# Attention scores of a hybrid encoder layer: fp32 on halves of the array in place of split fp32 on all of it

## The chip, the cores and the metric

The kernel runs on one core of a Trainium2 chip. A core has a matrix engine (TensorE, PE in the profile), a vector engine (VectorE, DVE), a scalar engine (ScalarE, ACT), a general engine (GpSimd, POOL) and a queue engine (SyncE, SP) that issues most transfers. Each engine takes its instructions in the order of the program and waits on semaphores for the others. The time is the device time of one execution in microseconds; a kernel's figure is the median of its runs.

## The reference

One layer of an encoder over two sequences (g = 0 and 1) of 2048 tokens with 1024 channels. One projection of the normalised input feeds three branches: a long convolution (hyena), a short convolution (conformer) and attention of the tokens to 256 memory tokens. Their gated outputs are joined, projected out and normalised again. What the change touches is the attention:

```
def memory_attention(q, mem_n, w_kv):
    k, v = jnp.split(mem_n @ w_kv, 2, axis=-1)      # 256 memory tokens
    q = q.reshape(B, L, 4, 64); k = k.reshape(B, M, 4, 64); v = ...
    s = jnp.einsum('blhd,bmhd->bhlm', q, k) * (64 ** -0.5)
    p = jax.nn.softmax(s, axis=-1)
    o = jnp.einsum('bhlm,bmhd->blhd', p, v)
```

All is in fp32. There are four heads of 64 channels, so two heads fill the 128 partitions.

## The kernel before

The kernel works in three stages. **Projections** (0 to 1381 us): for each block of 128 output channels the weights and the input are split into a high and a low part in a faster fp32 form (fp32r), and three matmuls (lines 416 to 418) per chunk give nearly fp32 results. Beside them run background jobs: keys and values of the memory (`kv_background`), the conformer's convolution (lines 215 to 257), the hyena filter (lines 295 to 334). **Attention** (1381 to 1542 us): 16 blocks of two heads by 512 queries (2 sequences, 2 pairs of heads, 4 token chunks), interleaved with the first transform of the long convolution (lines 799 to 809), two of its steps around each block. **Transforms and output**: the other transforms (lines 815 to 834) to about 1720 us, and then the output projection (lines 931 to 951).

In the projection stage `xa_q` scales a block of queries by 1/8 out of PSUM and splits it: the high part by ACT (L522), the low part by DVE (L523), and stores high and low of each head with four transfers (L526) so that a later load gives, for one head, high parts on partitions 0 to 63 and low parts on 64 to 127. `kv_background`'s `store` splits the transposed keys in the same way (lines 574 to 578). The high part of a key stands on all 128 partitions, the low part on 64 with zeros below. One full-array matmul with the high keys then adds high x high and low x high, a second with the low keys adds high x low.

An attention block goes in two halves of 256 queries (index `u`), and a half in two tiles of 128 queries (index `t`). For each tile: four matmuls into one PSUM bank (L748, two heads by two), the maximum by DVE (L752), two exps with sums by ACT (L756), the reciprocal by DVE (L758), the product by POOL (L760), four transposes by PE (L763) and one copy out of PSUM (L765). After both tiles, four output matmuls (L770), each with 64 columns of the array: head 0 gives partitions 0 to 63, head 1 64 to 127. These are plain fp32. Two PSUM banks hold scores (`ms`), three transposes (`tr`), one outputs (`po`).

The order of the instructions on each engine is not the order of the code alone: the tile framework's scheduler, with its own model of times, takes from what is ready. So an edit of one job can move others.

Of the kernel before, what the change touches and what calls it, by code (L numbers as in the profile page):

```python
# [18 lines left out]
P = 128  # L19
# [83 lines left out]
def kernel(ctx: ExitStack, tc: tile.TileContext, a: dict):  # L103
# [8 lines left out]
    dram = ctx.enter_context(tc.tile_pool(name="dram", bufs=1, space=bass.MemoryType.DRAM))  # L112
    HD = [[dram.tile([P, L + 2 * CH], F32, name=f"hd{g}{c}") for c in range(2)] for g in range(2)]
    SZ = [[dram.tile([P, L], F32, name=f"sz{g}{c}") for c in range(2)] for g in range(2)]
    QS = [[dram.tile([2, 64, 2, L], F32R, name=f"qs{g}{c}") for c in range(2)] for g in range(2)]
    ZX = [[dram.tile([P, L], F32, name=f"zx{g}{c}") for c in range(2)] for g in range(2)]
    KB = [dram.tile([P, 2048], F32R, name=f"kb{g}") for g in range(2)]
# [71 lines left out]
    with ExitStack() as c1:  # L189
# [328 lines left out]

        def xa_q(g, i):
            def f(tb, ps):  # L520
                qh, ql = sm(TB, F32R), sm(TB, F32R)
                nc.scalar.activation(qh, ps, AF.Copy, scale=0.125)  # L522
                nc.vector.scalar_tensor_tensor(ql, ps, 0.125, qh.bitcast(F32), op0=ALU.mult, op1=ALU.subtract)  # L523
                for j, q in enumerate((qh, ql)):
                    for h in range(2):
                        nc.sync.dma_start(QS[g][i][j, :, h, tb * TB:(tb + 1) * TB].bitcast(F32),  # L526
                                          q[64 * h:64 * h + 64, :].bitcast(F32))
            return (COL_Q + i * P, f)

        def kv_background():  # L530
            st = {}

            def norm(g):
                st["m", g] = big().rearrange("p (k t) -> p k t", k=KC)
                normed(st["m", g], a["mt"][g], mems[g][0], 8)
                st["p", g] = ms(), ms()

            def fetch(k):
                raw, wh, wl = sm(), bt(TB, F32R), bt(TB, F32R)
                nc.sync.dma_start(raw, a["xa_w_kv"][0, k * P:(k + 1) * P, :])  # L540
                split(wh, wl, raw)
# [12 lines left out]

            def store(g):
                kv = bt()
                vt = bt()
                vv = vt.rearrange("p (i m c) -> p i m c", i=2, m=2)
                for s, ps in enumerate(st["p", g]):
                    ss = slice(s * 256, (s + 1) * 256)  # L560
                    nc.scalar.copy(kv[:, ss], ps[:, 0:256])
                    nc.vector.tensor_copy(vv[:, :, s, :], ps[:, 256:512].rearrange("p (i c) -> p i c", i=2))
                nc.sync.dma_start(VT[g], vt)
                pk = tr()
                for i in range(2):
                    for s in range(2):
                        nc.tensor.transpose(pk[:, i * 256 + s * P:i * 256 + (s + 1) * P],
                                            kv[:, s * 256 + i * P:s * 256 + (i + 1) * P], ident)
                kt = big(2048, F32R)
                kb = kt.rearrange("p (h q m) -> p h q m", h=4, q=2)  # L570
                for h in range(4):
                    r = slice(64 * (h % 2), 64 * (h % 2) + 64)
                    ro = slice(64 - 64 * (h % 2), 128 - 64 * (h % 2))
                    src = pk[r, (h // 2) * 256:(h // 2 + 1) * 256]
                    nc.scalar.copy(kb[r, h, 0, :], src)
                    nc.scalar.copy(kb[ro, h, 0, :], src)
                    nc.vector.tensor_tensor(kb[0:64, h, 1, :], src, kb[r, h, 0, :].bitcast(F32), op=ALU.subtract)
                    nc.gpsimd.memset(kb[64:128, h, 1, :].bitcast(F32), 0.0)
                nc.sync.dma_start(KB[g].bitcast(F32), kt.bitcast(F32))

            bgq.append(lambda: norm(0))
            bgq.append(lambda: (norm(1), fetch(0)))
            for k in range(KC):
                bgq.append(lambda k=k: (fetch(k + 1) if k < KC - 1 else None, accum(k)))
            for g in range(2):
                bgq.append(lambda g=g: store(g))
# [108 lines left out]
    with ExitStack() as c2:  # L695
# [12 lines left out]
        kvs = {}  # L708

        def load_kv(g):  # L710
            kt, vt = ((woh[0:2], woh[3]), (wol[0:2], wol[2]))[g]
            for i in range(2):
                nc.gpsimd.dma_start(kt[i], KB[g][:, i * 1024:(i + 1) * 1024])
            vt = vt.bitcast(F32)[:, 0:512]
            nc.gpsimd.dma_start(vt, VT[g])
            kvs[g] = ([t.rearrange("p (h q m) -> p h q m", h=2, q=2) for t in kt],
                      vt.rearrange("p (i m c) -> p i m c", i=2, m=2))

        qn = [0]

        def queries(g, i, tb):
            qt = (woh[2], wol[5])[qn[0] % 2]
            qn[0] += 1
            nc.gpsimd.dma_start(qt.rearrange("p (h t) -> p h t", h=2),
                                QS[g][i][:, :, :, tb * TB:(tb + 1) * TB].rearrange("q r h t -> (q r) h t"))
            return qt

        pn = [0]
# [5 lines left out]
        def attention(g, i, tb, qy):  # L734
            kb, vt = kvs[g]
            qt = qy
            y = t_out()
            nc.sync.dma_start(y, ZX[g][i][:, tb * TB:(tb + 1) * TB])
            o = po_()
            for u in range(2):  # L740
                pt = pts[pn[0] % 6]
                pn[0] += 1
                for t in range(2):
                    sc = ms()
                    for h in range(2):
                        q0 = h * TB + u * 256 + t * P
                        for j in range(2):
                            nc.tensor.matmul(sc[:, h * 256:(h + 1) * 256], qt[:, q0:q0 + P], kb[i][:, h, j, :],  # L748
                                             start=j == 0, stop=j == 1)
                    mx = tiny.tile([P, 2], F32, tag="mx", name=nm("mx"))  # L750
                    se = tiny.tile([P, 2], F32, tag="se", name=nm("se"))
                    nc.vector.tensor_reduce(mx, sc.rearrange("p (h m) -> p h m", h=2), axis=AX.X, op=ALU.max,  # L752
                                            negate=True)
                    e = eps_[2 * u + t]
                    for h in range(2):
                        nc.scalar.activation(e[:, h * 256:(h + 1) * 256], sc[:, h * 256:(h + 1) * 256], AF.Exp,  # L756
                                             bias=mx[:, h:h + 1], accum_out=se[:, h:h + 1])
                    nc.vector.reciprocal(se, se)  # L758
                    ev = e.rearrange("p (h m) -> p h m", h=2)
                    nc.gpsimd.tensor_tensor(ev, ev, se.unsqueeze(2).broadcast_to([P, 2, 256]), op=ALU.mult)  # L760
                    tp = tr()
                    for k in range(4):
                        nc.tensor.transpose(tp[:, k * P:(k + 1) * P], e[:, k * P:(k + 1) * P], ident)  # L763
                    tv = tp.rearrange("p (k t) -> p k t", k=4)
                    (nc.vector.tensor_copy if t else nc.scalar.copy)(pt[:, :, t * P:(t + 1) * P], tv)  # L765

                for m in range(2):
                    for h in range(2):
                        hs = slice(64 * h, 64 * h + 64)
                        nc.tensor.matmul(o[hs, u * 256:(u + 1) * 256], vt[:, i, m, hs], pt[:, 2 * h + m, :],  # L770
                                         start=m == 0, stop=m == 1)
# [231 lines left out]
```

## Time and profile before

| | |
|---|---|
| runs | 2136.59 us median of 3 (2136.57 to 2137.94) |
| profiled execution | 2141.23 us, of which the span from first to last instruction is 2139.4 us |
| TensorE busy | 2005.3 us, 94% of the span, 9058 matmul records and as many weight loads |
| VectorE, ScalarE, GpSimd busy | 59%, 36%, 42% |
| mean granted TensorE clock | 0.975 |

Busy time is the sum of the records of an engine. Records of matmuls overlap (a matmul is recorded from its start to its modelled end, while the next has long begun), so the time that a matmul holds the engine is the distance from one start to the next, which the chain of waits shows. PEld is the weight load, which runs ahead of the matmul where it can. Idle time is given with what ended it.

### The profile page before, as it was taken

To read this page: it belongs to the slowest core of one execution; us is meant where nothing else is said; L and a number is where in the kernel's file an instruction comes from. 1 tells how busy PE (TensorE), PEld (TensorE's weight loads), DVE (VectorE), ACT (ScalarE), POOL (GpSimd) and SP (SyncE) were. 2 spreads that over 40 slices of the span, in tenths; PEclk is the share of its full clock that TensorE was granted. 3 is DMA by queue.
4 is the path that set the end of the run, shared out by engine and by line. 5 is a ranking of instruction groups with operands and counts; after the bars stand their busy time and mean duration, and the time that the engine had idled before them with its cause. 6 is when DMAs were issued, how large, how long until landed. Compare 5 with 4: busy or idle time off the path is not lost.

```text
span 2139.4 us, 26345 instructions
## 1 busy us (share of the span) xinstructions
PE 2005.3 (94%) x9058; PEld 1573.6 (74%) x9058; DVE 1266.4 (59%) x1747; ACT 761.6 (36%) x1439; POOL 897.6 (42%) x857
## 2 busy tenths in 40 slices
PE   5999998987999999998999899999988899999998
PEld 4888876776787788886777778777533278888886
DVE  5756397978315464469585963177887624333443
ACT  5531212231424233232233244277687711111211
POOL 3423475655533211455554541266588711111111
PEclk9999999999999999999999999999999989999999
DMA  9643222331657323222222236698788776555562
GB/s 334 206 149 137 90 99 89 109 109 69 220 169 230 125 100 109 86 90 81 95 80 105 81 114 204 218 296 259 236 263 272 229 194 155 154 144 152 148 151 56
DMA packets 197886, 331.81 MB, mean 155 GB/s; under 512 B 53129, under 2 KB 74265, under 8 KB 194938
## 3 DMA queue, kind: packets, MB, share of 16 engines
q1 hardware_dynamic: 170938, 272.06, 41.0%
q10 hardware_dynamic: 21392, 46.18, 6.6%
q0 software_dynamic: 5424, 11.90, 2.1%
q8 instruction: 72, 1.18, 0.2%
q14 instruction: 60, 0.49, 0.1%
HBM read 199.45 MB, written 130.61 MB: 154 GB/s over the span
## 4 chain that ended last, share of the span: by engine, by line
PE 49%; DVE 8%; DMA 4%; ACT 2%; issue 2%; POOL 2%; SPq 1%; ACTq 0%; POOLq 0%; DVEq 0%
PE pj L418 6%; PE pj L416 6%; PE pj L417 6%; PE ms L948 5%; PE ms L950 5%; PE ms L949 5%; DVE bg L220 5%; PE tr L931 2%; PE tr L763 1%; PE po L770 1%; PE ms L748 1%; PE tr L815 1%; DMA in<-xf 1%; PE ms L333 1%; DMA in<-x1d 1%
## 5 line engine op out<-in xcount | busy, mean ns | idle before, releaser
L416 PE MATMUL pj<-xh,whi 128*128 128x512 f32 (+1 forms) x1728 | 673.3, 390 | 29.0 <-ACT big L481 8.6
L417 PE MATMUL pj<-xl,whi 128*128 128x512 f32 (+1 forms) x1728 | 672.8, 389 | 7.8 <-POOL xl L387 5.1
L418 PE MATMUL pj<-xh,wlo 128*128 128x512 f32 (+1 forms) x1728 | 671.4, 389 | 0.0
L220 DVE SCALAR_TENSOR_TENSOR bg<-bg,vb,bg 128x512 f32<-128x512 f32 x480 | 420.4, 906 | 10.9 <-POOL bg L215 5.7
L416 PEld LDWEIGHTS pj<-xh,whi 128*128 128x128 f32 x1728 | 333.2, 193 | 98.9 <-ACT big L481 9.9
L417 PEld LDWEIGHTS pj<-xl,whi 128*128 128x128 f32 x1728 | 333.5, 193 | 73.2 <-POOL xl L387 5.9
L418 PEld LDWEIGHTS pj<-xh,wlo 128*128 128x128 f32 x1728 | 333.6, 193 | 65.1 <-DMA wlo<-ws 0.4
L948 PE MATMUL ms<-wo,mh 128*128 128x512 f32 x512 | 207.1, 405 | 1.8 <-ACT mh L178 1.8
L949 PE MATMUL ms<-wo,mh 128*128 128x512 f32 x512 | 201.7, 394 | 0.0
L950 PE MATMUL ms<-wo,ml 128*128 128x512 f32 x512 | 199.5, 396 | 0.2 <-POOL ml L179 0.2
L439 DVE SCALAR_TENSOR_TENSOR sm<-sm,va,sm 128x448 f32<-128x448 f32 (+1 forms) x96 | 82.4, 859 | 161.7 <-POOL sm L437 131.8
L437 POOL TENSOR_SCALAR sm<-sm,va 128x448 f32<-128x448 f32 (+1 forms) x96 | 113.0, 1178 | 135.6 <-ACT sm L430 129.2
L458 POOL TENSOR_TENSOR big<-big,sm 128x448 f32<-128x448 f32 (+1 forms) x64 | 121.5, 1899 | 107.7 <-DVE sm L441 104.2
L951 DVE TENSOR_TENSOR xr<-xr,ms 128x512 f32<-128x512 f32 x64 | 44.0, 687 | 204.3 <-PE ms L950 203.3
L185 POOL TENSOR_TENSOR ss<-ss,mhalf 128x1 f32<-128x1 f32 x32 | 17.6, 550 | 315.9 <-DVE ss L184 315.9
L183 ACT ACTIVATE junk<-xr 128x1024 bf16<-128x1024 f32 x32 | 33.8, 1058 | 318.4 <-DVE xr L951 318.2
L430 ACT COPY sm<-pj 128x512 f32<-128x512 f32 x96 | 56.1, 584 | 211.1 <-PE pj L418 162.9
L948 PEld LDWEIGHTS ms<-wo,mh 128*128 128x128 f32 x512 | 97.5, 191 | 21.4 <-ACT mh L178 3.2
L950 PEld LDWEIGHTS ms<-wo,ml 128*128 128x128 f32 x512 | 96.8, 189 | 21.2 <-POOL ml L179 0.6
L949 PEld LDWEIGHTS ms<-wo,mh 128*128 128x128 f32 x512 | 97.4, 190 | 19.2
L179 POOL TENSOR_TENSOR wlo<-sm,whi 128x512 fp32r<-128x512 f32 x50 | 77.7, 1567 | 73.4 <-ACT whi L178 70.6
L822 POOL TENSOR_TENSOR z<-z,us 128x512 f32<-128x512 f32 x64 | 81.4, 1282 | 30.8 <-DVE us L821 27.2
(177 smaller groups left out, 2935.0 us busy)
## 6 DMA issues: line engine op xcount, KB each, us to landing
big<-in_xt_dram SPq DMA_DIRECT2D x32, 512.0 KB, 5.5
in<-x1d SPq DMA_DIRECT2D x128, 128.0 KB, 3.7
aa<-o ACTq DMA_DIRECT2D x64, 256.0 KB, 3.7
at<-aa SPq DMA_DIRECT2D x64, 256.0 KB, 4.1
out_dram<-xr ACTq DMA_DIRECT2D x64, 256.0 KB, 3.6
sm<-in_win_dram SPq DMA_DIRECT2D x52, 256.0 KB, 3.3
ws<-whi SPq DMA_DIRECT2D x52, 256.0 KB, 2.1
ws<-wlo SPq DMA_DIRECT2D x52, 256.0 KB, 4.1
```

The source lines that it names most:

```text
L179: (sub_eng or nc.gpsimd).tensor_tensor(lo, src, hi.bitcast(F32), op=ALU.subtract)
L220: nc.vector.scalar_tensor_tensor(st["a", c], st["h", c][:, k:k + TB], vb[:, 2 * k + c:2 * k + c + 1], st["a", c], op0=ALU.mult, op1=ALU.add)
L416: nc.tensor.matmul(ps[:, ts_], hi, xh[:, k, ts_], start=k == 0, stop=False)
L417: nc.tensor.matmul(ps[:, ts_], hi, xl[:, k, ts_], start=False, stop=False)
L418: nc.tensor.matmul(ps[:, ts_], lo, xh[:, k, ts_], start=False, stop=k == KC - 1)
L437: nc.gpsimd.tensor_scalar(ct[:, o:e], pt[:, o + 1:e + 1], w[1], va[:, 52 + ch:53 + ch], op0=ALU.mult, op1=ALU.add)
L439: nc.vector.scalar_tensor_tensor(ct[:, o:e], pt[:, o:e], w[0], ct[:, o:e], op0=ALU.mult, op1=ALU.add)
L458: nc.gpsimd.tensor_tensor(v, v, out, op=ALU.mult)
L822: nc.gpsimd.tensor_tensor(z, z, us, op=op)
L948: nc.tensor.matmul(po, mh[:, k, :], woh[k][:, hs], start=i == 0, stop=False)
L949: nc.tensor.matmul(po, mh[:, k, :], wol[k][:, hs], start=False, stop=False)
L950: nc.tensor.matmul(po, ml[:, k, :], woh[k][:, hs], start=False, stop=i == 7)
```

## The change

The split of queries and keys is dropped. Queries are scaled and stored once (one transfer per chunk), keys are copied once. A score matmul now takes 64 partitions: head 0 on partitions 0 to 63, head 1 on 64 to 127, each head in a PSUM bank of its own, in plain fp32. A bank holds one head by 256 queries (two tiles) instead of two heads by 128 queries, and so do the maximum, the exps, the product and the transposes that follow; the loops over `t` and `h` change places. The buffers that queries, keys and values are loaded into move, and loads are smaller: 256 KB instead of 512 KB for queries, 256 KB instead of 1 MB for keys.

```diff
         def xa_q(g, i):
             def f(tb, ps):
-                qh, ql = sm(TB, F32R), sm(TB, F32R)
-                nc.scalar.activation(qh, ps, AF.Copy, scale=0.125)
-                nc.vector.scalar_tensor_tensor(ql, ps, 0.125, qh.bitcast(F32), op0=ALU.mult, op1=ALU.subtract)
-                for j, q in enumerate((qh, ql)):
-                    for h in range(2):
-                        nc.sync.dma_start(QS[g][i][j, :, h, tb * TB:(tb + 1) * TB].bitcast(F32),
-                                          q[64 * h:64 * h + 64, :].bitcast(F32))
+                q = sm()
+                nc.scalar.activation(q, ps, AF.Copy, scale=0.125)
+                nc.sync.dma_start(QS[g][i][:, tb * TB:(tb + 1) * TB], q)
...
-                kt = big(2048, F32R)
-                kb = kt.rearrange("p (h q m) -> p h q m", h=4, q=2)
-                for h in range(4):
...
-                    nc.scalar.copy(kb[r, h, 0, :], src)
-                    nc.scalar.copy(kb[ro, h, 0, :], src)
-                    nc.vector.tensor_tensor(kb[0:64, h, 1, :], src, kb[r, h, 0, :].bitcast(F32), op=ALU.subtract)
-                    nc.gpsimd.memset(kb[64:128, h, 1, :].bitcast(F32), 0.0)
-                nc.sync.dma_start(KB[g].bitcast(F32), kt.bitcast(F32))
+                kt = bt()
+                nc.scalar.copy(kt, pk)
+                nc.sync.dma_start(KB[g], kt)
...
+                sc = ms(), ms()
                 for t in range(2):
-                    sc = ms()
                     for h in range(2):
-                        q0 = h * TB + u * 256 + t * P
-                        for j in range(2):
-                            nc.tensor.matmul(sc[:, h * 256:(h + 1) * 256], qt[:, q0:q0 + P], kb[i][:, h, j, :],
-                                             start=j == 0, stop=j == 1)
+                        r, q0 = slice(64 * h, 64 * h + 64), u * 256 + t * P
+                        nc.tensor.matmul(sc[h][:, t * 256:(t + 1) * 256], qt[r, q0:q0 + P], kb[r, i, :],
+                                         start=True, stop=True)
+                for h in range(2):
...
-                    nc.vector.tensor_reduce(mx, sc.rearrange("p (h m) -> p h m", h=2), axis=AX.X, op=ALU.max,
+                    nc.vector.tensor_reduce(mx, sc[h].rearrange("p (t m) -> p t m", t=2), axis=AX.X, op=ALU.max,
...
-                    for k in range(4):
-                        nc.tensor.transpose(tp[:, k * P:(k + 1) * P], e[:, k * P:(k + 1) * P], ident)
-                    tv = tp.rearrange("p (k t) -> p k t", k=4)
-                    (nc.vector.tensor_copy if t else nc.scalar.copy)(pt[:, :, t * P:(t + 1) * P], tv)
+                    for m in range(2):
+                        for t in range(2):
+                            k = 2 * m + t
+                            nc.tensor.transpose(tp[:, k * P:(k + 1) * P], e[:, t * 256 + m * P:t * 256 + (m + 1) * P],
+                                                ident)
+                    (nc.vector.tensor_copy if h else nc.scalar.copy)(
+                        pt[:, 2 * h:2 * h + 2, :], tp.rearrange("p (m t) -> p m t", m=2))
```

The change moves instructions on PE too. Lines have other numbers in the changed kernel: L732 are the scores (before L748), L737 the maximum (L752), L743 the reciprocal (L758), L750 the transposes (L763), L758 the outputs (L770), L787 and L793 to L795 the transform's transposes and matmuls (L799, L805 to L807). In the rows below `ms` is a score bank, `po` the output bank, `tr` and `pa` banks of transposes and transforms, `x4` four calls in a row; a plain fp32 call is one row here.

PE in the kernel before, in the second half of a block in the steady part of the attention stage: the scores of both tiles stand together.

```order
L799 MATMUL tr_10974<-ident,u_1514_10851 128x128 x4
L748 MATMUL ms_11075<-wo_9935,wo_9947 128x256 x4
L748 MATMUL ms_11093<-wo_9935,wo_9947 128x256 x4
L799 MATMUL tr_11008<-ident,u_1552_10997 128x128 x4
L770 MATMUL po_10888<-ynp,wo_9937 64x256 x4
L763 MATMUL tr_11047<-ident,ynp 128x128 x4
```

PE in the changed kernel, at the same place; bank 10903 is head 0 and bank 10904 head 1.

```order
L787 MATMUL tr_10806<-ident,u_1498_10691 128x128 x4
L732 MATMUL ms_10903<-wo_9824,wo_9833 128x256 x2
L758 MATMUL po_10728<-ynp,wo_9825 64x256
L787 MATMUL tr_10840<-ident,u_1536_10829 128x128 x4
L732 MATMUL ms_10904<-wo_9824,wo_9833 128x256 x2
L758 MATMUL po_10728<-ynp,wo_9825 64x256 x3
L750 MATMUL tr_10880<-ident,ynp 128x128 x4
```

The scores of the two heads are parted by an output matmul and four transposes, and the four output matmuls are parted into one and three.

PE in the kernel before, in the first half of the same block.

```order
L748 MATMUL ms_11035<-wo_9935,wo_9947 128x256 x4
L748 MATMUL ms_11053<-wo_9935,wo_9947 128x256 x4
L805 MATMUL pa_10871<-k_1519_10867,th_10858 128x512
L806 MATMUL pa_10871<-k_1519_10867,tl_10859 128x512
L807 MATMUL pa_10871<-k_1520_10868,th_10858 128x512
L805 MATMUL pa_10878<-k_1519_10867,th_10858 128x512
L806 MATMUL pa_10878<-k_1519_10867,tl_10859 128x512
L807 MATMUL pa_10878<-k_1520_10868,th_10858 128x512
L763 MATMUL tr_10941<-ident,ynp 128x128 x4
L770 MATMUL po_10888<-ynp,wo_9937 64x256 x4
```

PE in the changed kernel, in the first half of that block; bank 10867 is head 0 and bank 10868 head 1.

```order
L732 MATMUL ms_10867<-wo_9824,wo_9833 128x256 x2
L732 MATMUL ms_10868<-wo_9824,wo_9833 128x256 x2
L750 MATMUL tr_10778<-ident,ynp 128x128 x4
L758 MATMUL po_10728<-ynp,wo_9825 64x256
L793 MATMUL pa_10711<-k_1503_10707,th_10698 128x512
L794 MATMUL pa_10711<-k_1503_10707,tl_10699 128x512
L795 MATMUL pa_10711<-k_1504_10708,th_10698 128x512
L793 MATMUL pa_10718<-k_1503_10707,th_10698 128x512
L794 MATMUL pa_10718<-k_1503_10707,tl_10699 128x512
L795 MATMUL pa_10718<-k_1504_10708,th_10698 128x512
L750 MATMUL tr_10791<-ident,ynp 128x128 x3
L758 MATMUL po_10728<-ynp,wo_9825 64x256 x3
```

Here the scores stay together, head 0 twice and then head 1 twice, and the outputs are parted again.

DVE in the kernel before, at the end of the projections: the last low halves of queries (L523) stand ahead of the first maximum (L752).

```order
L616 COPY sm_9661<-ms_9657 128x512
L523 SCALAR_TENSOR_TENSOR sm_9817<-pj_9791,sm_9816 128x512
L523 SCALAR_TENSOR_TENSOR sm_9850<-pj_9824,sm_9849 128x512
L523 SCALAR_TENSOR_TENSOR sm_9883<-pj_9857,sm_9882 128x512
L523 SCALAR_TENSOR_TENSOR sm_9916<-pj_9890,sm_9915 128x512
L752 TENSOR_REDUCE mx_10015<-ms_10010 128x2
```

DVE in the changed kernel, at the same place (L604 is the transform's copy, before L616).

```order
L179 TENSOR_TENSOR bg_9564<-tr_9558,bg_9563 128x512
L604 COPY sm_9548<-ms_9544 128x512
L604 COPY sm_9571<-ms_9567 128x512
L737 TENSOR_REDUCE mx_9905<-ms_9899 128x2
L737 TENSOR_REDUCE mx_9918<-ms_9900 128x2
```

The four rows are gone, and the maxima of the first half block follow the transform's copies directly.

## Rows read from the trace of the kernel before

**Rows 1.** The page: engines (busy, share, count), and the chain that ended last.

```profile
PE 2005.3 (94%) x9058; PEld 1573.6 (74%) x9058; DVE 1266.4 (59%) x1747; ACT 761.6 (36%) x1439; POOL 897.6 (42%) x857
...
PE 49%; DVE 8%; DMA 4%; ACT 2%; issue 2%; POOL 2%; SPq 1%; ACTq 0%; POOLq 0%; DVEq 0%
```

**Rows 2.** Busy time by stretch: length, engines' busy us (count), granted clock, DMA share, GB/s.

```profile
76.00:306.00 230.00, 230.00 (x1078) 192.28 (x1076) 144.23 (x193) 60.65 (x115) 101.62 (x96) 1.00 0.36 124
1400.00:1496.00 96.00, 96.00 (x674) 75.27 (x673) 74.19 (x148) 74.82 (x238) 60.78 (x70) 1.00 0.94 276
...
1386.00:1390.00 4.00, 3.38 (x15) 2.80 (x14) 1.94 (x6) 2.04 (x8) 3.47 (x4) 0.50 0.99 321
```

**Rows 3.** The chain of waits through one attention block: start us, us, what.

```profile
1449.01 0.44 PE tr L763 x4
1449.45 0.96 PE ms L748 x8
1450.40 0.23 PE pa L805
...
1451.79 0.44 PE tr L763 x4
1452.23 1.01 PE po L770 x8
1453.24 0.59 PE tr L763 x4
1453.83 0.44 PE tr L799 x4
1454.27 0.96 PE ms L748 x8
1455.22 0.44 PE tr L799 x4
1455.66 1.01 PE po L770 x8
1456.67 0.59 PE tr L763 x4
...
1458.65 0.44 PE tr L763 x4
```

**Rows 4.** The chain behind the attention, and line 295's matmuls (min/median/max ns, starts).

```profile
1538.85 0.86 PE ms L829 x2
...
L295 PE MATMUL ms<-f,wf x48: 377/378/792, 697.9 to 1271.8; 128*128 128x256 f32 x32, 66*128 66x256 f32 x16
```

**Rows 5.** Lines 748 and 770: weight loads (min/median/max ns, first to last start).

```profile
L748 PEld LDWEIGHTS ms<-wo,wo x256: 186/190/338, 1380.9 to 1531.9; 128*128 128x128 f32 x128
...
L770 PEld LDWEIGHTS po<-ynp,wo x256: 132/136/138, 1393.4 to 1542.2; 128*64 128x64 f32 x128
```

**Rows 6.** PE's waits in the projections: waiting <- waited for, us, times, longest.

```profile
PE ms L228 <- ACT bg L178: 21.4, 3, 9.2
...
PE pj L416 <- ACT big L481: 8.6, 3, 4.3
...
PE pj L416 <- ACT sm L430: 6.5, 3, 3.6
...
PE pj L416 <- DVE sm L523: 4.8, 4, 1.7
```

**Rows 7.** PE's three longest waits from 1381 to 1545 us.

```profile
PE ms L748 <- ACT ynp L756: 2.2, 4, 0.9
PE ms L748 <- DVE sm L523: 0.9, 1, 0.9
PE tr L763 <- POOL ynp L760: 0.4, 1, 0.4
```

**Rows 8.** Line 523: its instructions, and what DVE was idle for before them (us, times).

```profile
L523 DVE SCALAR_TENSOR_TENSOR sm<-pj,sm x16: 680/691/693, 634.2 to 1382.0; 128x512 fp32r<-128x512 f32 x16
...
  ACT sm L522: 66.0, 8
```

**Rows 9.** Line 577, the subtractions of the key preparation.

```profile
L577 DVE TENSOR_TENSOR big<-tr,big x8: 404/418/427, 141.7 to 149.4; 64x256 fp32r<-64x256 f32 x8
```

More of the change, by code (lines that the diff above doesn't have):

```diff
@@ L114 @@
     SZ = [[dram.tile([P, L], F32, name=f"sz{g}{c}") for c in range(2)] for g in range(2)]
-    QS = [[dram.tile([2, 64, 2, L], F32R, name=f"qs{g}{c}") for c in range(2)] for g in range(2)]
+    QS = [[dram.tile([P, L], F32, name=f"qs{g}{c}") for c in range(2)] for g in range(2)]
     ZX = [[dram.tile([P, L], F32, name=f"zx{g}{c}") for c in range(2)] for g in range(2)]
-    KB = [dram.tile([P, 2048], F32R, name=f"kb{g}") for g in range(2)]
+    KB = [dram.tile([P, 512], F32, name=f"kb{g}") for g in range(2)]
     VT = [dram.tile([P, 512], F32, name=f"vt{g}") for g in range(2)]
@@ L568, in store @@
                                             kv[:, s * 256 + i * P:s * 256 + (i + 1) * P], ident)
-                kt = big(2048, F32R)
-                kb = kt.rearrange("p (h q m) -> p h q m", h=4, q=2)
-                for h in range(4):
-                    r = slice(64 * (h % 2), 64 * (h % 2) + 64)
-                    ro = slice(64 - 64 * (h % 2), 128 - 64 * (h % 2))
-                    src = pk[r, (h // 2) * 256:(h // 2 + 1) * 256]
-                    nc.scalar.copy(kb[r, h, 0, :], src)
-                    nc.scalar.copy(kb[ro, h, 0, :], src)
-                    nc.vector.tensor_tensor(kb[0:64, h, 1, :], src, kb[r, h, 0, :].bitcast(F32), op=ALU.subtract)
-                    nc.gpsimd.memset(kb[64:128, h, 1, :].bitcast(F32), 0.0)
-                nc.sync.dma_start(KB[g].bitcast(F32), kt.bitcast(F32))
+                kt = bt()
+                nc.scalar.copy(kt, pk)
+                nc.sync.dma_start(KB[g], kt)
             bgq.append(lambda: norm(0))
@@ L710, in load_kv @@
         def load_kv(g):
[L711 to L714, printed above, removed]
+            kt, vt = (t.bitcast(F32)[:, 0:512] for t in (woh[2 * g], woh[2 * g + 1]))
+            nc.gpsimd.dma_start(kt, KB[g])
             nc.gpsimd.dma_start(vt, VT[g])
-            kvs[g] = ([t.rearrange("p (h q m) -> p h q m", h=2, q=2) for t in kt],
-                      vt.rearrange("p (i m c) -> p i m c", i=2, m=2))
+            kvs[g] = (kt.rearrange("p (i m) -> p i m", i=2), vt.rearrange("p (i m c) -> p i m c", i=2, m=2))
         qn = [0]
         def queries(g, i, tb):
-            qt = (woh[2], wol[5])[qn[0] % 2]
+            qt = wol[qn[0] % 2].bitcast(F32)[:, 0:TB]
             qn[0] += 1
-            nc.gpsimd.dma_start(qt.rearrange("p (h t) -> p h t", h=2),
-                                QS[g][i][:, :, :, tb * TB:(tb + 1) * TB].rearrange("q r h t -> (q r) h t"))
+            nc.gpsimd.dma_start(qt, QS[g][i][:, tb * TB:(tb + 1) * TB])
             return qt
@@ L750, in attention @@
+                for h in range(2):
                     mx = tiny.tile([P, 2], F32, tag="mx", name=nm("mx"))
                     se = tiny.tile([P, 2], F32, tag="se", name=nm("se"))
-                    nc.vector.tensor_reduce(mx, sc.rearrange("p (h m) -> p h m", h=2), axis=AX.X, op=ALU.max,
+                    nc.vector.tensor_reduce(mx, sc[h].rearrange("p (t m) -> p t m", t=2), axis=AX.X, op=ALU.max,
                                             negate=True)
-                    e = eps_[2 * u + t]
@@ L755, in attention @@
-                    for h in range(2):
-                        nc.scalar.activation(e[:, h * 256:(h + 1) * 256], sc[:, h * 256:(h + 1) * 256], AF.Exp,
-                                             bias=mx[:, h:h + 1], accum_out=se[:, h:h + 1])
+                    e = eps_[2 * u + h]
+                    for t in range(2):
+                        nc.scalar.activation(e[:, t * 256:(t + 1) * 256], sc[h][:, t * 256:(t + 1) * 256], AF.Exp,
+                                             bias=mx[:, t:t + 1], accum_out=se[:, t:t + 1])
@@ L758, in attention @@
                     nc.vector.reciprocal(se, se)
-                    ev = e.rearrange("p (h m) -> p h m", h=2)
+                    ev = e.rearrange("p (t m) -> p t m", t=2)
                     nc.gpsimd.tensor_tensor(ev, ev, se.unsqueeze(2).broadcast_to([P, 2, 256]), op=ALU.mult)
                     tp = tr()
-                    for k in range(4):
-                        nc.tensor.transpose(tp[:, k * P:(k + 1) * P], e[:, k * P:(k + 1) * P], ident)
-                    tv = tp.rearrange("p (k t) -> p k t", k=4)
@@ L765, in attention @@
-                    (nc.vector.tensor_copy if t else nc.scalar.copy)(pt[:, :, t * P:(t + 1) * P], tv)
+                    for m in range(2):
+                        for t in range(2):
+                            k = 2 * m + t
[3 more added lines that the diff above has]
+                        pt[:, 2 * h:2 * h + 2, :], tp.rearrange("p (m t) -> p m t", m=2))
```

## The prediction

> **What bounds the kernel now.** I read the profile from the outside in. The page first: TensorE (PE) is busy 94% of the span, and the chain that ended last is half PE [rows 1]. Then busy time by stretch: the attention stage, which the change rewrites, has its first score at 1381 us and its last output at 1542 us [rows 5], and between 1400 and 1496 us PE is busy 96.00 of 96.00 us at granted clock 1.00 (the upper of its two levels, 2.4 GHz), while VectorE (DVE) has 74, ScalarE (ACT) 75 and GpSimd (POOL) 61 us of work [rows 2]. A busy PE is not proof, so third the chain of waits over one round: one block from 1449.01 to 1458.65 us, 9.64 us, is PE instructions one behind the other with nothing between them [rows 3]. The reader is to see that the pieces add up to the round (two score groups of 0.96, two output groups of 1.01, transposes of 0.44 or 0.59, twelve passes of 0.23): whatever this stage adds to PE lengthens the kernel, and whatever it saves elsewhere does not shorten it.
>
> **What a pass costs.** A plain fp32 matmul is two passes: the filter's matmul on line 295 runs 24 times and shows 48 records, and the two of a 128x512 one hold PE 0.86 us [rows 4]. So a pass over 512 columns is 0.43 us and one over 256 is 0.215. A split-fp32 (fp32r) matmul is one pass; eight with 256 columns take 0.96 us with their weight loads, 0.12 each [rows 3]. Fewer rows do not make a pass shorter: 16 of line 295's 48 records have 66 rows instead of 128, and none is under 377 ns at a median of 378 [rows 4].
> The output matmul (L770) already is plain fp32 on halves of the array (64 columns each). Its eight passes would be 1.72 us in a row, but take 1.01: the two halves work side by side, 4 x 0.215 = 0.86, and 0.15 more for getting in. The transposes behind it take 0.59 where they otherwise take 0.44 [rows 3]: 0.15 more for getting out.
>
> **The scores.** Per half block of 256 queries (32 in the program) the old kernel has eight passes of 0.12; the new one has four matmuls, so also eight passes, but of 0.215: 0.86 us if the two row halves run side by side all the way, 1.72 if not. Against 0.96 that alone would be near nothing. The order decides. Two places of it stand with the change. In the second half of a block the scheduler puts an output matmul and transposes between the scores of head 0 and those of head 1, so they cannot run side by side. Counted over the whole order, 17 of the 32 half blocks are parted like this (1.72 each, 29.2 us), 13 have head 0 twice and then head 1 twice, one alternates (0.86), one is parted by half (1.29). For the 13 the ends are 0.86 (the second half starts while the first still has passes queued) and 1.72 (it waits); no row has such a sequence, and I take the middle, 1.29. Sum 29.2 + 0.9 + 1.3 + 16.8 = 48.2, with ends 42.6 and 53.8; before 32 x 0.96 = 30.7. **Plus 17.5 us** (11.9 to 23.1).
> The Trainium skill ("TensorE: Matmul & The Clock Gate", Part 3, The mechanism) says that matmuls start and end strictly in order, and only weight loads run ahead. By that only one pass of the 13 would overlap, 7 x 0.215 = 1.51 each, and the term would be 20.3; no run here shows it for row halves.
>
> **The outputs.** The softmax tile used to hold both heads of 128 queries and now holds one head of 256, so the first output matmul (head 0, keys 0 to 127) is ready before the rest and the scheduler issues it alone. Alone it is two passes with nothing beside them, 0.43; the other three take 0.86, since head 1 has four passes in them. That is 31 half blocks x 0.43 = **plus 13.3 us**.
>
> **Getting in and out of halves.** Before, the order has 33 groups on halves (all L770), 32 of them left for full-array work. After it has 48 groups of row halves and 63 of column halves, entered 111 times and left for full-array work 71 times (31 times a row group is followed by a column group directly). (78 + 39) x 0.15 = 17.6 us; and a row half is entered with a weight load of 128 columns instead of 64, 190 against 136 ns [rows 5], 48 x 0.054 = 2.6. **Plus 20.2 us.** The price is that of column halves; rows show none for row halves, so its ends are 20.2 and what is left if row groups are free: 9.2 (56 crossings and the 2.6 less).
> The Trainium skill ("TensorEngine Tiling (Array Packing)", Key Properties) says that a change of tiling mode drains the engine, with no exception for row tiling. By it the 20.2 stands; the trace agrees for columns, with the 0.15 us on each side.
>
> **What is saved.** The query's low half (L523, 0.69 us on DVE, 16 times) is gone. PE waited for it four times in the projections, 4.8 us in all [rows 6]; late next is ACT's copy (L522), for which L523 itself waits [rows 8], so I count 4 x 0.69 = 2.8 (ends 0 and 4.8). At the start of attention the second score group waits 0.9 us for the last L523 [rows 7]; now it waits for the ACT copy alone, 0.7 saved. The DVE place with the change shows that row gone ahead of the first maximum. Everything else I put at nothing: the key preparation (8 ACT copies, 4 subtractions and 4 memsets a group become one copy) lies at 141 to 150 us [rows 9], under PE busy 230.00 of 230.00 us [rows 2]; the three query stores less per tile (SP) and the smaller loads on POOL's queue lie under a PE that does not wait for a DMA in the attention stage [rows 7]. If that cover went, they would be worth a few us more. The pieces of softmax (maximum, exp, reciprocal, product, copy) keep count and size.
> **New waits.** Both score banks are now filled at once, so scores of the next half block need both exp pairs done. Between two uses of a bank lie some 6 us of PE work in the new order, and maximum and exps take about 2 us, so I put nothing; the upper end is twice today's 3.5 us of PE waits in this stage [rows 7], 7.0.
>
> **Sum.** 17.5 + 13.3 + 20.2 - 2.8 - 0.7 = +47.5 us, on a round of 9.64 some 3 more. The profiled execution took 2141.2 us (span 2139.4), the median of the runs is 4.6 lower: 2136.6 + 47.5 = 2184 us. The lower end of the terms that are measured in kind: 11.9 + 13.3 + 20.2 - 4.8 - 0.9 = +39.7; the upper 23.1 + 13.3 + 20.2 + 7.0 - 0.7 = +62.9.
>
> **Rivals.**
> 1. *Row groups cross for free.* Only column groups pay, and the row halves overlap fully: 11.9 + 13.3 + 9.2 - 3.5 = +31, 2168 us. For it: no row shows the row price. Against: the column price is regular, 0.15 at every group of rows 3.
> 2. *A new chain of waits.* PE stands still for exp at the parted scores. With 0.5 to 1 us per half block on top of the sum, +64 to +80, 2200 to 2216. For it: PE waited 0.9 us for exp at the very start of the stage [rows 7]. Against: other engines have a fifth of the round free and the round grows.
> 3. *The clock falls.* The granted clock was 0.50 from 1386 to 1390 us, behind PE's waits [rows 2], and a stage full of half-array passes might hold it at 1.2 GHz. A third of a stage of some 190 us at half speed costs about 60 more: 2245. Against: it stays 1.00 through today's half-array groups.
> 4. *Not slower: the projections give it back.* PE's waits there for ACT's and DVE's evictions and for the conformer's means add up to 21.4 + 8.6 + 6.5 + 4.8 = 41.3 us [rows 6]. Without L523's, which is counted, 36.5 remain. If the lighter ACT and DVE of the first 150 us took all of them away, +39.7 becomes +3 and rival 1's +31 becomes -5.5: 2131 to 2140 us. It decides only if those waits hang on work that the change lightens; against it, PE is solid from 76 to 306 us [rows 2], so the delay does not reach back to the key preparation, and PE's order in the projections is unchanged around those matmuls.
>
> **How the numbers follow.** Forecast 2184 (its own range 2172 to 2204) 68%; rival 1 14%; rival 2 8%; rival 3 3%; rival 4 7%. A measurement tells 0.2%, 4 us, from no change. Faster is half of rival 4 and a little of what I did not see, 5%; within 0.2% 4%; slower 91%. The range from 2160 to 2205 holds the forecast and rival 1.
>
> **What would show it.** Right: a round of 12 to 13 us in the steady stage with PE still without gaps; the parted score groups 0.86 us plus 0.15 to 0.2; single output matmuls of 0.43 with transposes of 0.59 behind; 0.86 to 1.72 for the adjacent scores. Rival 1: transposes behind a score group at 0.44. Rival 2: idle PE before scores, ended by ACT. Wrong altogether if PE's busy share in the stage falls, or the round stays under 10 us.

## The result, and the profile after

The changed kernel takes 2196.8 us (median of 4 runs, 2194.6 to 2200.6) against 2136.6 us beside it (4 runs, 2136.0 to 2137.9): ratio 1.027, 95% interval 1.026 to 1.029. The profiled execution took 2200.6 us, with a span of 2198.9 us (2139.4 before), 59.5 us more.

Three marks part that span: the first score, the last output, the end. Before they stand at 1381.1, 1542.8 and 2139.4 us, after at 1398.0, 1604.3 and 2198.9. So the projections ahead of the attention lose 16.9 us, the attention stage 44.7 (206.4 in place of 161.7), and what comes behind gains 2.1.

**Attention.** The chain of waits of the changed kernel through adjacent and parted half blocks (start us, us, what):

```profile
1491.82 1.06 PE ms L732 x4
1492.88 0.57 PE po L758 x2
1493.46 0.59 PE tr L787 x4
1494.04 1.06 PE ms L732 x4
1495.10 1.01 PE po L758 x6
...
1498.51 1.06 PE ms L732 x4
...
1505.27 1.07 PE ms L732 x8
1506.34 0.58 PE po L758 x2
...
1510.92 1.07 PE ms L732 x8
1511.99 0.59 PE tr L750 x4
...
1516.77 1.06 PE ms L732 x4
```

This answers to [rows 3]. Four half blocks lie between 1491.82 and 1516.77 us, so a block takes 12.48 us where it took 9.64. Eight passes on both row halves (x8) take 1.07 us, four passes on one half (x4) 1.06: half the work at the same price. The whole stage has 34 groups of four, which are the 17 parted half blocks, and 11 groups of eight; the first three half blocks stand together at its start. A single output matmul (po x2) takes 0.57 or 0.58, and transposes behind a score group 0.59.

PE has no gap in it. Busy time by stretch (length, PE, PEld, DVE, ACT, POOL, granted clock, DMA share, GB/s), and PE's waits in the stage:

```profile
76.00:306.00 230.00, 223.88 (x1041) 186.85 (x1042) 128.03 (x176) 55.33 (x101) 109.19 (x84) 0.99 0.33 115
...
1500.00:1560.00 60.00, 60.00 (x331) 38.92 (x330) 36.77 (x73) 36.57 (x116) 28.15 (x33) 1.00 0.52 160
```

```profile
PE ms L732 <- ACT ynp L741: 1.4, 1, 1.4
```

The other engines became lighter per unit of time (DVE 37 of 60 us, where it had 74 of 96 in [rows 2]); in this stretch the stage is PE's work alone, and the clock is at its upper level. The fence of waits is all that the view lists for PE from 1398 to 1606 us.

**Projections.** The first row above is the sign: 230.00 busy us of 230.00 before [rows 2], 223.88 now. Which waits came in, from PE's waits ahead of the attention (waiting <- waited for: us, times, longest):

```profile
PE ms L228 <- ACT bg L178: 23.7, 3, 9.2
PE pj L416 <- ACT big L481: 12.2, 4, 3.7
...
PE pj L418 <- POOL wlo L179: 6.1, 1, 6.1
```

The first two were 21.4 and 8.6 [rows 6]; L523's 4.8 are gone. The third row is new. It stands at 180.9 us. If each matmul of lines 416 to 418 is set beside the one of the same number in the kernel before, it starts 0.4 us later ahead of this wait and 8.5 behind it. The 8.1 us are more than the wait of 6.1: behind it matmuls follow each other in 0.43 us in place of 0.23, at a granted clock of 0.54 in the mean, close to the lower of the two levels (1.2 GHz), where the kernel before had 1.00. The same happens behind the second place, which is described below (length, PE, PEld, DVE, ACT, POOL, clock, DMA share, GB/s):

```profile
187.00:191.00 4.00, 3.98 (x10) 3.17 (x11) 3.86 (x5) 0.00 (x0) 1.65 (x1) 0.54 0.54 207
722.00:727.00 5.00, 4.80 (x12) 3.83 (x13) 5.00 (x6) 1.12 (x2) 3.22 (x2) 0.54 0.86 306
```

GpSimd (POOL) in the changed kernel ahead of the first place (start, us, instruction, idle time before and what ended it):

```profile
143.44 0.78 POOL L215 TENSOR_SCALAR bg<-bg,vb 128x512 f32<-128x512 f32 x1 [5.69 <-DMA bg<-hd]
154.17 1.12 POOL L215 TENSOR_SCALAR bg<-bg,vb 128x512 f32<-128x512 f32 x1 [9.96 <-DVE big L504]
...
165.50 23.15 POOL L179 TENSOR_TENSOR wlo<-sm,whi 128x512 fp32r<-128x512 f32 x2 [10.21 <-DMA sm<-in_win_dram]
```

Two subtractions of 128x512 take 23.15 us. The first alone takes 21.46 (6.86 in the kernel before); others of that form take 1.29. What VectorE (DVE) does beside it, in the changed kernel (165.5 to 185.1 us) and then in the kernel before (168.2 to 173.3 us):

```profile
165.21 20.63 DVE L220 SCALAR_TENSOR_TENSOR bg<-bg,vb,bg 128x512 f32<-128x512 f32 x31
...
167.94 6.05 DVE L220 SCALAR_TENSOR_TENSOR bg<-bg,vb,bg 128x512 f32<-128x512 f32 x9
```

These are taps of the conformer's convolution. In both kernels they start 0.66 us apart, each before the last has ended. What differs is how long that goes on: such taps end at 185.8 us now and at 174.0 before, and the subtraction ends 1.1 us behind them in both. L215 opens a channel of the convolution. Before, its channels start at 137.66 and 159.48 us, so that the first is nearly done when the second joins; now at 143.44 and 154.17, and the taps of both stand together for longer. The first channel starts late because its load stands later in SP's queue (before, then now):

```profile
134.24 0.38 SPq L213 DMA_DIRECT2D bg<-hd  x1
...
138.88 0.32 SPq L567 DMA_DIRECT2D kb<-bg  x1
...
140.41 0.38 SPq L213 DMA_DIRECT2D bg<-hd  x1
```

It now comes behind the store of the keys (L567).

The second place is at 710 to 722 us in the changed kernel, with 4.6 and 3.1 us of PE's waits for weights. The chain there:

```profile
705.33 6.38 DMA big<-in_xt_dram
...
711.73 1.65 DVE big L367 x4
713.38 1.84 DVE xl L387
715.22 0.02 SPq L357
...
716.17 0.38 SPq L405
...
716.65 5.52 DMA wlo<-ws
...
722.20 0.80 PE pj L416
```

The weight load (L405) is issued right behind an input load (L357) that stood until a large buffer came free; SP takes its transfers in order. PE starts as soon as the weight has landed.

The listed waits ahead of the attention add up to 89.0 us before and 104.2 now. Of the growth of 3.6 and 2.3 us in the first two rows no run here shows the cause, and none shows that of the 2.1 us gained behind the attention.

### The profile page after: what moved, and what is told of

Read it like the earlier page. It is cut to its first block, busy times and chain, and to the rows that moved or that the text cites. A ratio compares the mean times of both kernels' runs of the same rounds, so it can differ in the third digit from the quotient of the medians.

```text
span 2198.9 us, 26250 instructions
## 1 busy us (share of the span) xinstructions
PE 2052.2 (93%) x9058; PEld 1583.7 (72%) x9058; DVE 1250.5 (57%) x1723; ACT 759.1 (35%) x1427; POOL 908.9 (41%) x847
## 4 chain that ended last, share of the span: by engine, by line
PE 60%; DVE 17%; DMA 8%; issue 6%; POOL 5%; ACT 3%; SPq 1%; ACTq 0%; POOLq 0%; DVEq 0%
DVE bg L220 10%; PE pj L417 9%; PE pj L418 9%; PE pj L416 9%; PE ms L936 5%; PE ms L938 5%; PE ms L937 5%; DMA bg<-in_x_sample_dram 3%; PE ms L732 3%; PE tr L919 2%; PE po L758 2%; PE tr L750 2%; DVE sm L439 1%; POOL wlo L179 1%; DVE big L367 1%
## 5 line engine op out<-in xcount | busy, mean ns | idle before, releaser
L416 PE MATMUL pj<-xh,whi 128*128 128x512 f32 (+1 forms) x1728 | 675.6, 391 | 35.2 <-ACT big L481 12.2
L220 DVE SCALAR_TENSOR_TENSOR bg<-bg,vb,bg 128x512 f32<-128x512 f32 x480 | 415.6, 901 | 9.1 <-POOL bg L215 4.7
L179 POOL TENSOR_TENSOR wlo<-sm,whi 128x512 fp32r<-128x512 f32 x50 | 91.2, 1840 | 73.9 <-ACT whi L178 57.8
L937 PEld LDWEIGHTS ms<-wo,mh 128*128 128x128 f32 x512 | 96.8, 189 | 19.0
L745 POOL TENSOR_TENSOR ynp<-ynp,se 128x512 f32<-128x512 f32 x64 | 66.2, 1038 | 64.1 <-DVE se L743 62.8
```

The lines of the kernel that those rows point to most:

```text
L179: (sub_eng or nc.gpsimd).tensor_tensor(lo, src, hi.bitcast(F32), op=ALU.subtract)
L220: nc.vector.scalar_tensor_tensor(st["a", c], st["h", c][:, k:k + TB], vb[:, 2 * k + c:2 * k + c + 1], st["a", c], op0=ALU.mult, op1=ALU.add)
L416: nc.tensor.matmul(ps[:, ts_], hi, xh[:, k, ts_], start=k == 0, stop=False)
L937: nc.tensor.matmul(po, mh[:, k, :], wol[k][:, hs], start=False, stop=False)
```

## The experiments

My theory after the result: (A) the attention loses by half-array groups that stand apart (halves without a partner, and each group's way in and out), and the projections lose by where the key and query edits put buffers and transfers. The rival (B) is that fp32 scores as such, or other work, are the cost. Ratios are against the kernel before on the same chip.

**out_grouped.** One loop turned round, so that the output matmul that is ready last is asked for first:

```diff
                 for m in range(2):
-                    for h in range(2):
+                    for h in (1, 0):
```

> The changed kernel with one edit: the four output matmuls of a query block are issued head 1 first, so that all four are ready together and none of the 31 single ones is left (32 groups of four in place of 31 of one and 31 of three). The sections of the array's use fall by 42, from 182 to 140. Theory A (what costs is every score or output group that stands alone, and every crossing): 31 x 0.43 = 13.3 us and 42 x 0.15 to 0.2 = 6.3 to 8.4 us come back; first score to last output falls from 206.0 to some 184 to 187 us, the whole from 2196.8 to 2175 to 2178. Theory B (the time is in the fp32 scores themselves, and the single output only stands where PE would have stood anyway): the stage stays within 3 us of 206 and the whole above 2192.

Measured: 2184.3 us, ratio 1.0188 (1.016 to 1.022), against 1.027 for the change; the stage takes 185.1 us. Its chain:

```profile
1495.17 1.07 PE ms L732 x8
1496.24 0.58 PE tr L750 x4
...
1498.66 1.01 PE po L758 x8
1499.67 0.59 PE tr L787 x4
1500.26 1.06 PE ms L732 x4
```

The stage falls as theory A has it: 206.4 - 185.1 = 21.3 us. Counted from a group's first start to the next group's, the output groups hold PE 32.5 us in place of 50.1, so 17.6 of it is there: the single ones, with their way in. The total is some 6 us above the forecast's upper end: that chip's kernel before was at 2142.2, and the projections' loss is still there (6.1 us at 179 us). The totals forecast here and below start from 2196.8 us, which was measured on another chip, so stages and ratios are the fairer comparison.

**keys_big.**

```diff
-                kt = bt()
+                kt = big(TB)
```

> The changed kernel with one word undone: the tile into which the keys are copied comes from the pool of large buffers again, not from the pool of six. The order of matmuls in the attention is that of the changed kernel. Theory A (the keys take the fifth and sixth buffer of the pool, the convolution's loads wait for one, its two channels' taps then alternate on VectorE without a gap, and GpSimd's subtraction beside them takes 21.5 us): the convolution's loads are issued some 10 us earlier again, the subtraction is back at some 7 us, the wait of 6.1 us for its tile near 181 us is gone and the first score stands at some 1390 in place of 1398.0; the whole falls by 7 to 9 us to 2188 to 2190. Theory B (the projections are late for another reason, for instance the query tiles that are no longer split): the wait stays, the whole stays within 2 us of 2196.8.

Measured: 2189.5 us, ratio 1.022 (1.019 to 1.025). First score at 1388.6, PE busy 229.47 of the 230 us from 76 to 306. GpSimd now:

```profile
137.39 0.77 POOL L215 TENSOR_SCALAR bg<-bg,vb 128x512 f32<-128x512 f32 x1 [0.75 <-DMA bg<-hd]
153.45 0.77 POOL L215 TENSOR_SCALAR bg<-bg,vb 128x512 f32<-128x512 f32 x1 [15.29 <-DMA bg<-hd]
...
164.44 10.34 POOL L179 TENSOR_TENSOR wlo<-sm,whi 128x512 fp32r<-128x512 f32 x2 [10.21 <-ACT whi L178]
```

The first channel starts 6 us earlier, its load being issued at 133.9 us ahead of the key store, the subtraction is at 8.64 us in place of 21.46, and the wait is gone. Theory A holds; B's "the wait stays" does not. One point of A is put otherwise by the traces: no wait for a buffer is recorded at the load; it has another place in SP's queue.

**before_third_buffer**, the same from the other side: the kernel before, with a sixth buffer taken.

```diff
+                kx = bt()
+                nc.scalar.copy(kx, pk)
+                nc.sync.dma_start(KX[g], kx)
```

> The kernel before the change, with one thing added: each sequence's key projection is also copied by ScalarE into a tile from the pool of six and stored to a place that nothing reads, so that keys, weights and values of two sequences take all six buffers, as they do after the change. Its attention is untouched. Theory A (the sixth buffer delays the convolution's first load, and the rest follows): the convolution's taps start alternating between channels, GpSimd's subtraction of 128x512 near 166 us takes some 20 us in place of 6.9, PE waits some 6 us for its tile near 181 us, and the first score comes at 1388 to 1391 in place of 1381; the whole is 7 to 10 us up. Theory B (that wait of after comes from the unsplit queries or from less work on VectorE): the subtraction stays near 7 us and the first score within 2 us of 1381.

Measured: 2144.0 us, ratio 1.0028 (1.0016 to 1.0041), about 6 us. GpSimd in it, and PE's waits from 160 to 230 us:

```profile
160.31 0.77 POOL L216 TENSOR_SCALAR bg<-bg,vb 128x512 f32<-128x512 f32 x1 [21.41 <-DMA bg<-hd]
162.79 1.29 POOL L216 TENSOR_SCALAR bg<-bg,vb 128x512 f32<-128x512 f32 x1 [1.71 <-DVE bg L221]
165.36 3.02 POOL L180 TENSOR_TENSOR wlo<-sm,whi 128x512 fp32r<-128x512 f32 x2 [1.28 <-ACT whi L179]
187.17 16.68 POOL L180 TENSOR_TENSOR wlo<-sm,whi 128x512 fp32r<-128x512 f32 x1 [18.79 <-ACT whi L179]
```

```profile
PE pj L419 <- POOL wlo L180: 1.2, 1, 1.2
```

The mechanism comes as expected, though not at the subtraction that was expected: both channels start together, the ones near 166 us pass in 3.02, and a later one takes 16.7 us. The price does not: it falls on a tile that is needed later, PE waits 1.2 us instead of some 6, and the first score comes at 1383.2, 2 us late. The held-up subtraction is shown from both sides; what it costs depends on which weight it hits. The rest of the 6 us is spread over the stages and not explained.

**q_low_kept.** The query's low half is computed and stored as before the change (nothing reads it):

```diff
+                nc.vector.scalar_tensor_tensor(ql, ps, 0.125, q, op0=ALU.mult, op1=ALU.subtract)
+                for d, t in ((QS, q), (QL, ql)):
+                    for h in range(2):
+                        nc.sync.dma_start(d[g][i][64 * h:64 * h + 64, tb * TB:(tb + 1) * TB], t[64 * h:64 * h + 64, :])
```

> The changed kernel in which VectorE still computes the low half of each query tile and the query is still stored in four half stores, high and low, as before the change; nothing reads the low halves. Theory A (with these stores gone the order of SyncE's queue around the cross attention's query moved, and a weight load stands behind an input load that waits for a buffer: 4.6 + 3.1 us of PE's waits at 710 to 722 us): these waits are gone, the first score stands some 6 us earlier, at 1391 to 1393. Its order in the attention differs from that of the changed kernel (55 score groups of two in place of 34), so its stages are compared and not its whole. Theory B (the removed subtractions and stores cost nothing and their absence delays nothing): the first score stays within 2 us of 1398, or comes later by the wait of 4.8 us for the subtraction that was there before.

PE's waits from 700 to 735 us:

```profile
PE pj L417 <- DMA whi<-ws: 1.1, 1, 1.1
PE pj L417 <- DVE sm L524: 1.0, 1, 1.0
```

2.1 us in place of 7.7, as in the kernel before. But the subtraction's own waits are back (5.2 us from 380 us on, 4.8 before), and the first score gains only 3.2 us, to 1394.7: theory A has the wait right and the first score too early. That gain is no more than runs with the changed kernel's projections differ among themselves (1393.9 to 1401.6).

The delay of each matmul of lines 416 to 418 against the one of the same number in the kernel before separates the two places better. The step near 181 us is 7.9 to 8.6 us in all five runs of the changed kernel with the keys in the pool of six, and 0.0 in the three with the keys in a large buffer (keys_big, out_keys, s2_tr2_all). Between the matmuls that the kernel before starts at 600 and at 735 us the delay grows by 4.4 to 6.5 us in all six runs without the query's extra stores, and by 0.9 and 0.6 in the two that keep them (q_low_kept, s2_tr2_all). Both of these also keep the subtraction; that it is the stores rests on the chain at 705 to 722 us.

The whole, 2205.9 us (ratio 1.028, 1.024 to 1.032), says nothing on this question: its attention has 55 score groups of two matmuls in place of 34, and takes 215.8 us. That is 9.4 us more with no edit in the attention itself, which fits theory A on parted halves.

**all_grouped.** out_grouped, and both score banks in one tile, so that four scores are ready together. There is only one such tile, so a half block's scores also wait until both banks of the last one are free:

```diff
-                sc = ms(), ms()
+                s2 = mk[0]()
+                sc = s2[:, 0:TB], s2[:, TB:2 * TB]
```

> The changed kernel with the outputs in groups of four, as in out_grouped, and both heads' scores in one tile of two banks, so that the four score matmuls of a block are ready together too (30 groups of four and one of eight, in place of 34 of two, 11 of four and some others). 125 sections in place of 182. Theory A (parted halves and crossings): the scores take 32 x 0.86 = 27.5 us in place of some 42, the single outputs' 13.3 us are gone, and 57 crossings x 0.15 to 0.2 = 8.6 to 11.4: the stage falls from 206.0 to some 166 to 170 us (161.5 before the change), the whole to 2157 to 2161. It stays above before, since 31 score groups still cross into and out of halves of the array, which cost before nothing. Theory B (scores in one tile wait for both heads' exponentials, where each bank came free by itself): a wait of up to 1 us in most of 32 blocks shows in PE's waits at the scores, the stage stays at 185 us or more.

Measured: 2194.5 us, ratio 1.0235 (1.021 to 1.026), stage 197.5 us. PE's waits in the stage:

```profile
PE po L762 <- DVE ynp L756: 13.2, 17, 1.1
PE tr L754 <- POOL ynp L749: 8.0, 24, 0.5
PE s L736 <- ACT ynp L745: 4.8, 2, 3.9
PE s L736 <- issue: 2.2, 1, 2.2
```

```profile
sum 200.00, PE 169.92 PEld 108.62 DVE 121.56 ACT 125.48 POOL 98.17; mean PE 33.98 PEld 21.72 DVE 24.31 ACT 25.10 POOL 19.63
```

The second fence is busy time from 1400 to 1600 us. Theory A has the work right (169.9 us of PE, 166 to 170 forecast) and the time wrong: 28 us of waits came in. Its chain goes from the scores through maximum, exps, product, transposes and copies, round after round: PE is no longer the bound. Theory B was right that waits come in and that the stage stays above 185 us, though most waits stand at the outputs and transposes and not at the scores.

**s2_tr2.** all_grouped with two such tiles; two banks are taken from transposes and products.

```diff
-        tr, pa, po_ = psum(c2, tr=3, pa=2, po=1)
+        tr, pa, po_ = psum(c2, tr=2, pa=1, po=1)
...
-        s2p = cs.enter_context(tc.tile_pool(reuse_waits="tile", name="s2p", bufs=1, space=PS))
+        s2p = cs.enter_context(tc.tile_pool(reuse_waits="tile", name="s2p", bufs=2, space=PS))
```

> all_grouped with two of its two-bank score tiles in place of one; the two banks for that are taken from the transposes (two in place of three) and from the Fourier stage's products (one in place of two). Theory A (the 28 us of PE's waits in all_grouped's attention come from the single score tile, with which only one block is in flight): the waits at the outputs (13.2 us) and transposes (8.0 us) go, what is left is PE's work of some 170 us, the stage at 168 to 173, the whole at 2160 to 2168. Theory B (they come from the order that PE's instructions are in, whatever the buffers, or the taken banks make new waits at transposes and products): the stage stays above 185 us.

Measured: 2201.4 us, ratio 1.030 (1.028 to 1.032), stage 194.7 us. PE's waits from 1385 to 1600 us:

```profile
PE s L736 <- ACT ynp L745: 13.1, 11, 3.0
PE pa L797 <- ACT us L801: 4.3, 6, 0.7
...
PE pa L797 <- DVE us L801: 1.7, 5, 0.3
```

The waits at outputs and transposes are gone, as A said, but others stand at the scores and, with one bank for products, there; the part behind the attention is 13 us longer too. A's time is refuted and B's stage above 185 us holds. Of B's reasons the products' bank is seen, with 6.0 us; what is behind the 13.1 us at the scores is open. That the single tile was all of the wait in all_grouped is not shown, since the taken banks changed two things at once.

**out_keys.** The edits of out_grouped and keys_big together.

> The two edits out_grouped and keys_big together. If the two losses are independent, the gains add: the stage from first score to last output at 185 us as in out_grouped, no wait for GpSimd's tile near 181 us, first score at 1388 to 1390, the whole at 2167 to 2174, about 1.4 to 1.6% above before. If they are one loss (the order in the attention already repaired by either), the whole stays at 2178 or more.

Measured: 2168.9 us, ratio 1.0151 (1.013 to 1.018); first score 1386.8, stage 184.5. The two losses are apart, and add.

**s2_tr2_all.** s2_tr2 with the edits of keys_big and q_low_kept.

> Everything together: the grouped scores in two tiles of two banks as in s2_tr2, the grouped outputs, the keys in large buffers as in keys_big, and the query's low halves computed and stored (and read by nothing) as in q_low_kept. If the named causes are all there is: first score at 1382 to 1388, the stage at 168 to 173, the rest 595, together 2147 to 2156, 0.5 to 1% above before: the scores' 31 crossings into and out of halves of the array, 31 x (0.2 + 0.15) = 10.9 us, are left, and cost more than the 30.7 - 27.5 = 3.2 us that fp32 scores save. If fp32 scores on half arrays were worth having, it would be below 2136.

Measured: 2186.2 us, ratio 1.022 (1.020 to 1.025); first score 1385.3 as forecast, stage 194.2 and 608.9 behind it, both as in s2_tr2. So repairing the projections works here too; the attention misses, and what follows it too, as in s2_tr2. No version that ran beats the kernel before; out_keys is the nearest, 1.5% above.

## Why the prediction was right, and where it was wrong

The direction, the range and most of the mechanism held: 2196.8 us lies between 2160 and 2205. The forecast of 2184 was 12.8 us too low, and two errors of opposite sign stand behind that.

- *The scores, +17.5: mis-sized.* I took the middle, 1.29 us, for the 13 adjacent half blocks. The 11 of them that stand by themselves in the trace take 1.07, which is the lower end, 0.86, and 0.2 for getting in. The term is 11.9. The Trainium skill ("TensorE: Matmul & The Clock Gate", Part 3, The mechanism) speaks of matmuls in strict order, from which I had worked out 1.51 for them; the 1.07 us contradict that reading for row halves. The parted halves came as said, 0.86 and 0.2.
- *The outputs, +13.3: right.* Single ones take 0.57, that is 0.43 and 0.15, and with the outputs in groups of four (out_grouped) they are gone.
- *Crossings, +20.2: right in kind, and so rival 1 falls.* Transposes behind scores take 0.59, as behind column groups in [rows 3], and a score group takes 0.2 over its passes. The Trainium skill ("TensorEngine Tiling (Array Packing)", Key Properties) says that a change of tiling mode drains the engine; the trace agrees, for rows and columns, with these 0.15 and 0.2 us at a change. With 11.9 the attention terms are 11.9 + 13.3 + 20.2 - 0.7 = 44.7; measured are 44.7. That they meet to a tenth is luck. Counted from a group's first start to the next group's, scores hold PE 41.5 us before and 59.5 after, outputs 32.6 and 50.1, everything else 87.5 and 96.8: +18.0, +17.5 and +9.3, where the terms with their crossings give 21.7, 17.8 and 5.9. Two misses of some 3.5 us cancel.
- *New waits, 0 with 7.0 as upper end: right.* 1.4 us, where it was 3.5 [rows 7]. Rival 2 did not come in the changed kernel. It came in all_grouped and s2_tr2, where PE's work was less and the score tiles were changed: it sits close behind PE's bound.
- *"Everything else I put at nothing": the step that failed.* The key preparation's work is hidden under a busy PE, as said. But I priced its instructions and left out two things the diff shows: the tile moved into the pool of six that the convolution also loads into, and without the query's stores SP's queue runs in another order. Both move places in SP's queue, which the prediction had set aside because PE was busy above the work. The first costs 8.1 us near 181 us and nothing where the keys are in a large buffer (keys_big, out_keys, s2_tr2_all; before_third_buffer gives the mechanism, at a smaller price). The second costs 4.7 us by 735 us, and under 1 where the stores are kept (q_low_kept, s2_tr2_all). Together they are 12.8 of the 16.9 us; the other 4.1 stay unexplained. Part of each is the lower clock behind the wait.
- *L523, -2.8: right in kind, but drowned.* Its waits of 4.8 us are gone, and 1.2 us for ACT's copy (L522) came, as said; but the projections as a whole are 16.9 us later, not 2.8 earlier.
- *Rival 3* falls, with a clock of 1.00 from 1500 to 1560 us and 0.98 over the whole stage, as before the change. *Rival 4* falls the other way: the two largest waits it hoped to see shrink grew (23.7 against 21.4, 12.2 against 8.6 us).

Made up again: 47.5, less 5.6 for the scores, plus 19.7 for the projections (16.9 and the 2.8 not gained), less the 2.1 behind the attention, gives 59.5; the spans differ by 59.5. This is a balance of measured stages and no check of the causes: the total is off by less than its largest term, because 5.6 us too much in the scores stand against 19.7 too little in the projections.

## What to carry to other kernels

In this kernel halves of the array paid only in pairs: ask for each row or column group whether its partner will be ready at the same moment, since a half alone cost as much as both (1.06 and 1.07 us), and each group paid its way in and out. Where one engine is full, a group that waits for its partner may cost more in latency than it saves in work. An edit whose work is hidden still moves buffers and places in a queue: read from which pool its tiles come, who else takes from it, and what its removed transfers stood in front of.

## What the runs showed of the hardware

A GpSimd subtraction of 128x512 that takes 1.29 us with VectorE idle was held for as long as VectorE's taps started 0.66 us apart, each before the last had ended. It took 21.46 us (the changed kernel), 21.04 (out_grouped), 16.68 (before_third_buffer), 8.64 (keys_big) and 6.86 (the kernel before), and in all five it ended 1.1 to 1.2 us behind the last of these taps. The two taps that follow, 35 ns apart from their neighbours, take some 1.65 us in place of 0.74, beside the end of one subtraction and the next. The Trainium skill ("Trainium Architecture — The Big Picture", What this means for kernel authors) says that these two engines share a pair of ports under an exclusive lock. The trace fits a lock rather than a shared rate. Which engine gets in is not settled: in before_third_buffer a subtraction at 165.36 us, near the start of such a row of taps, took 1.32 us, and a tap beside it 1.78. That a gap between dependent taps is what lets GpSimd in at the end is argued, not shown.

Fp32 matmuls on the two row halves overlap fully when head 0's two are queued ahead of head 1's two: eight passes in 1.07 us, four in 1.06. The passes of the two heads start in turn, 13 to 14 ns apart.
